# FFN gate and up projections by seven products of quarters, weight sums on the vector engine, and the FFN in three parts

## The chip, the core and the metric

The kernel runs on one core of one Trainium2 chip. A core has a tensor engine (PE: matrix products and transposes, which write to PSUM), a vector engine (DVE), a scalar engine (ACT), GpSimd (POOL) and a sync engine (SP), whose queue issues the transfers here. SBUF is the working memory, PSUM the eight banks in which products are accumulated. The metric is device time in microseconds (us) of one execution; lower is better.

## What is computed

A trunk of two layers over 512 tokens of width 1024, all in float32. Each layer has four sub-layers, each of them normalised before and after and added to the residual stream `h`: a feed-forward network (FFN), a mixer (convolution and gated spatial mixing in layer 0, causal pooling in layer 1), cross-attention over 256 memory tokens, and a second FFN.

```
def swiglu_ffn(h, w_gu, w_down):            # h: 512 x 1024, w_gu: 1024 x 5632, w_down: 2816 x 1024
    gu = h @ w_gu
    gate, up = jnp.split(gu, 2, axis=-1)
    return (jax.nn.silu(gate) * up) @ w_down

for i in range(DEPTH):                      # DEPTH = 2
    f = swiglu_ffn(rms_norm(h, ffn1_pre_g[i]), ffn1_w_gu[i], ffn1_w_down[i])
    h = h + 0.5 * rms_norm(f, ffn1_post_g[i])
    hn = rms_norm(h, mix_pre_g[i])
    m = even_mixer(hn, ...) if i % 2 == 0 else odd_mixer(hn, ...)
    h = h + rms_norm(m, mix_post_g[i])
    c = memory_cross_attention(rms_norm(h, xa_pre_g[i]), mem, ...)
    h = h + rms_norm(c, xa_post_g[i])
    f = swiglu_ffn(rms_norm(h, ffn2_pre_g[i]), ffn2_w_gu[i], ffn2_w_down[i])
    h = h + 0.5 * rms_norm(f, ffn2_post_g[i])
```

## The kernel before, in words

**Split operands.** Every operand of a large product is held as a high part in a short float format (fp32r) and a low part, the exact rest: `split` has ACT write the high part (a cast, L72) and DVE the low part (a subtraction, L73). `mm3` (L75 to L78) then issues three matmuls for one product: high by high, high by low, low by high. Weights come from memory by SP into a `raw` tile (two buffers of 1 MB), and are split into `whi` and `wlo` (five buffers each, `N_W`, of 128 x 1024). Activations lie features-on-partitions in `big` tiles (thirteen buffers).

**Gate and up.** `ffn` goes over 22 blocks of 128 hidden features two at a time. For each pair, `fm_quad` makes four outputs of 128 features by 512 tokens: two of gate, two of up. Each output is eight steps of 128 rows of the weight, each step three matmuls of 512 columns, so 24 matmuls an output and 96 a quad. ACT then takes silu of gate (L322), DVE multiplies by up (L323), and `split` makes the hidden activation. The first quad of a sub-layer runs in two halves of 256 tokens, with the transposes of the later token tiles between them (`pre.turn()`).

**Down.** The hidden features go in two parts, of 12 and of 10 blocks. After the first part, `w_down`'s first twelve blocks are multiplied in: the first 512 output columns are copied to `f`, the second 512 stay open in PSUM (`accs1`). `tm_out` does the last part, with the norm after it: token tile by token tile it squares (L293), scales (L294), adds to `h` (L306), and starts the next sub-layer's norm (`nxt.tile`, `rms_transpose`): square (L127), a root on POOL (L119), scaling by root and gain on DVE (L137), transposes on PE (L144), split. `TAIL` keeps the last eight steps of the second half of the columns in token order, so that the norms of early tiles run under the products of later ones.

**PSUM.** Four banks in pool `pa` (`psa`), two in `pb` (`psb`), two in `pt` (`pst`, and `tps` for transposes).

**Order.** A scheduler sets each engine's order from the program and its estimates of durations; each engine then runs its own list strictly in order, waiting by semaphores for what its instructions need. A tile's buffer is given out again when its last reader has finished.

Of the kernel before, what the change touches and what calls it, by code (L numbers as in the profile page):

```python
# [4 lines left out]
F32 = mybir.dt.float32  # L5
# [5 lines left out]
P = 128  # L11
# [14 lines left out]
N_Q = 3  # L26
N_W = 5
TAIL = 8
CUTS = (0, 4)
TURNS = (0, 2)  # L30


def trunk_kernel(tc, x, mem, ffn1_pre_g, ffn1_w_gu, ffn1_w_down, ffn1_post_g,
# [8 lines left out]
    with ExitStack() as es:  # L42
# [7 lines left out]
        pa = es.enter_context(tc.tile_pool(name="pa", bufs=4, space=bass.MemoryType.PSUM))  # L50
        pb = es.enter_context(tc.tile_pool(name="pb", bufs=2, space=bass.MemoryType.PSUM))
# [9 lines left out]
        # ---------------------------------------------------------- helpers  # L61
# [13 lines left out]
        def mm3(ps, lhs, rhs, start, stop):  # L75
            nc.tensor.matmul(out=ps, lhsT=lhs[0], rhs=rhs[0], start=start, stop=False)  # L76
            nc.tensor.matmul(out=ps, lhsT=lhs[0], rhs=rhs[1], start=False, stop=False)  # L77
            nc.tensor.matmul(out=ps, lhsT=lhs[1], rhs=rhs[0], start=False, stop=stop)  # L78
# [19 lines left out]

        def gain(g, tag):
            gb = gp.tile([P, D], F32, name=tag, tag=tag)  # L100
            nc.sync.dma_start(out=gb, in_=g.partition_broadcast(P))
            return gb

        def gain_by_pe(g, tag):
            """The same spread over partitions by the tensor engine, from one row."""
            row = qt([P, D])
            nc.sync.dma_start(out=row[:1, :], in_=g[None, :])
            one = cst.tile([1, P], F32, name="one")
            nc.vector.memset(one, 1.0)
            gb = gp.tile([P, D], F32, name=tag, tag=tag)  # L110
            for c in (0, 512):
                ps = psb()
                nc.tensor.matmul(out=ps, lhsT=one, rhs=row[:1, c:c + 512], start=True, stop=True)
                nc.vector.tensor_copy(gb[:, c:c + 512], ps)
            return gb
# [6 lines left out]
        def rms_transpose(src, gb, dsts):  # L122
# [17 lines left out]
            def turn():  # L140
                for i in range(2):
# [3 lines left out]
                    split(dsts[i][0], dsts[i][1], tps)  # L145
            return turn

        class Prenorm:
            def __init__(self, g, w, c0s, by_pe=False):
                self.gb = (gain_by_pe if by_pe else gain)(g, "pre")  # L150
                self.x = Act()
                self.turns = []
                self.first = (w, c0s)
                self.ws = None
# [5 lines left out]
            def tile(self, t):  # L160
                self.turns.append(rms_transpose(h[:, t, :], self.gb,
                                                [self.x.block(i, t * P, (t + 1) * P) for i in range(2)]))

            def turn(self):
                self.turns.pop(0)()

# [14 lines left out]
        def w_fm_load(w, c0, parts=1):  # L181
            raw = wp.tile([P, KD, 256], F32, name="raw", tag="raw", bufs=2)
            n = 256 // parts
            return raw, [lambda i=i: nc.sync.dma_start(
                out=raw[:, :, i * n:(i + 1) * n],
                in_=w[:, c0 + i * n:c0 + (i + 1) * n].rearrange("(k p) n -> p k n", p=P)) for i in range(parts)]

        def w_fm(w, c0, raw=None):
# [593 lines left out]
```

## Time and profile before

| | us |
|---|---|
| median of 3 runs (2084.77 to 2086.85) | 2085.42 |
| span of the profiled execution | 2082.8 |
| PE busy in it | 2048.0 (98%) |
| DVE busy | 958.7 (46%) |
| ACT busy | 723.0 (35%) |
| POOL busy | 70.9 (3%) |

The profile is of one execution; its span runs from the first to the last instruction, 2.6 us less than the median time. Matmuls are pipelined, so a matmul's own duration (0.39 us for 512 columns) is longer than the distance from one start to the next, and it is that distance which counts. A group of equal instructions has its count, its busy time and the mean duration of one. An idle time stands with the instruction that ended it.

### The profile page before, as it was taken

The page shows a single profiled execution, that of the slowest core. Times are in us where ns is not written, and L with a number is a line of the kernel's source. Part 1 is how long each engine was busy: PE and PEld are TensorE (multiplying, and loading weights), DVE is VectorE, ACT ScalarE, POOL GpSimd, SP SyncE. Part 2 cuts the span into 40 slices and gives each one's busy share as a digit, 9 for nine tenths or more (in the row PEclk, how much of TensorE's full clock was granted, in tenths as well). Part 3 has the DMA queues.
Part 4 walks back from the last instruction along what each step waited for, and adds up shares of the span by engine and source line. Part 5 has one row for each costly group of instructions (what it writes and reads, how often), then busy time and mean ns, then how long its engine had stood idle before and what let it go on. Part 6 is the DMA issues. An engine that isn't in the chain of part 4 may idle for free.

```text
span 2082.8 us, 24330 instructions
## 1 busy us (share of the span) xinstructions
PE 2048.0 (98%) x10158; PEld 1732.2 (83%) x10158; DVE 958.7 (46%) x1343; ACT 723.0 (35%) x1113; POOL 70.9 (3%) x101
## 2 busy tenths in 40 slices
PE   8999999998999999999999999999999999999998
PEld 7888888887878888888888888888888888888887
DVE  5332233699956463323336332233676654322333
ACT  5222332434454452322224322222444443322221
POOL 0000000112010010000001000000001000000000
PEclk9999999999999999999999999999999999999999
DMA  6223223333632133233223332322352113323221
GB/s 224 85 100 101 90 93 101 118 98 105 224 140 102 66 99 103 98 101 101 96 87 102 102 101 101 101 88 95 102 182 96 67 63 115 97 101 101 98 95 51
DMA packets 165189, 218.17 MB, mean 105 GB/s; under 512 B 3741, under 2 KB 124085, under 8 KB 164056
## 3 DMA queue, kind: packets, MB, share of 16 engines
q1 hardware_dynamic: 163928, 208.24, 30.2%
q0 software_dynamic: 1152, 8.39, 1.0%
q8 instruction: 79, 1.29, 0.3%
q14 instruction: 30, 0.25, 0.0%
HBM read 210.33 MB, written 6.29 MB: 104 GB/s over the span
## 4 chain that ended last, share of the span: by engine, by line
PE 86%; DVE 7%; ACT 2%; POOL 2%; issue 2%; DMA 1%; POOLq 0%; DVEq 0%; ACTq 0%
PE psa L78 13%; PE psa L77 13%; PE psa L76 13%; PE psb L76 11%; PE psb L77 11%; PE psb L78 11%; PE pst L76 4%; PE pst L78 4%; PE pst L77 4%; POOL r L119 1%; DVE q L137 1%; DVE big L483 1%; DVE wlo L73 1%; DVE h L306 1%; PE tps L144 1%
## 5 line engine op out<-in xcount | busy, mean ns | idle before, releaser
L72 ACT CAST whi<-raw 128x1024 fp32r<-128x1024 f32 x370 | 388.1, 1053 | 1114.9 <-PE psb L77 365.9
L73 DVE TENSOR_TENSOR wlo<-raw,whi 128x1024 fp32r<-128x1024 f32 x370 | 452.2, 1225 | 694.9 <-ACT whi L72 686.9
L76 PE MATMUL psb<-big,whi 128*128 128x512 f32 (+1 forms) x1120 | 397.3, 355 | 8.5 <-DVE big L73 8.5
L77 PE MATMUL psb<-big,whi 128*128 128x512 f32 (+1 forms) x1120 | 396.4, 354 | 0.1
L78 PE MATMUL psb<-big,wlo 128*128 128x512 f32 (+1 forms) x1120 | 396.0, 354 | 0.0
L76 PE MATMUL psa<-whi,big 128*128 128x512 f32 x896 | 350.8, 392 | 0.0
L77 PE MATMUL psa<-wlo,big 128*128 128x512 f32 x896 | 349.3, 390 | 0.0
L78 PE MATMUL psa<-whi,big 128*128 128x512 f32 x896 | 348.5, 390 | 0.5 <-DVE big L73 0.5
L76 PEld LDWEIGHTS psb<-big,whi 128*128 128x128 f32 x1120 | 212.7, 190 | 39.5 <-issue 7.8
L77 PEld LDWEIGHTS psb<-big,whi 128*128 128x128 f32 x1120 | 212.8, 190 | 29.3 <-DVE big L73 0.7
L78 PEld LDWEIGHTS psb<-big,wlo 128*128 128x128 f32 x1120 | 212.7, 190 | 28.9
L76 PE MATMUL psa<-big,whi 128*128 128x512 f32 (+1 forms) x656 | 228.6, 349 | 0.0
L78 PE MATMUL psa<-big,wlo 128*128 128x512 f32 (+1 forms) x656 | 228.2, 348 | 0.0
L77 PE MATMUL psa<-big,whi 128*128 128x512 f32 (+1 forms) x656 | 228.1, 348 | 0.0
L78 PEld LDWEIGHTS psa<-whi,big 128*128 128x128 f32 x896 | 168.2, 188 | 35.8 <-DVE big L73 0.9
L76 PEld LDWEIGHTS psa<-whi,big 128*128 128x128 f32 x896 | 168.2, 188 | 35.5 <-ACT big L72 0.8
L77 PEld LDWEIGHTS psa<-wlo,big 128*128 128x128 f32 x896 | 168.2, 188 | 34.1
L78 PEld LDWEIGHTS psa<-big,wlo 128*128 128x128 f32 x656 | 124.1, 189 | 15.6
L76 PEld LDWEIGHTS psa<-big,whi 128*128 128x128 f32 x656 | 124.2, 189 | 15.5
L77 PEld LDWEIGHTS psa<-big,whi 128*128 128x128 f32 x656 | 124.2, 189 | 15.4
L76 PE MATMUL pst<-big,whi 128*128 128x512 f32 x320 | 124.5, 389 | 0.0
L77 PE MATMUL pst<-big,whi 128*128 128x512 f32 x320 | 124.5, 389 | 0.0
(161 smaller groups left out, 1847.0 us busy)
## 6 DMA issues: line engine op xcount, KB each, us to landing
raw<-in_ffn_w_gu_dram SPq DMA_DIRECT2D x86, 1024.0 KB, 5.0
raw<-in_ffn_w_down_dram SPq DMA_DIRECT2D x40, 1024.0 KB, 5.0
raw<-in_xa_w_kv_dram SPq DMA_DIRECT2D x16, 1024.0 KB, 5.4
raw<-in_ev_w_in_dram SPq DMA_DIRECT2D x8, 1024.0 KB, 5.4
raw<-in_xa_w_q_dram SPq DMA_DIRECT2D x8, 1024.0 KB
raw<-in_xa_w_o_dram SPq DMA_DIRECT2D x8, 1024.0 KB, 6.2
raw<-in_ffn_w_down_dram SPq DMA_DIRECT2D x8, 512.0 KB, 3.6
kv<-big POOLq DMA_DIRECT2D x4, 1024.0 KB, 8.0
```

What stands on the lines that cost most here:

```text
L72: nc.scalar.copy(out=hi, in_=src)
L73: nc.vector.tensor_tensor(out=lo, in0=src, in1=hi.bitcast(F32), op=ALU.subtract)
L76: nc.tensor.matmul(out=ps, lhsT=lhs[0], rhs=rhs[0], start=start, stop=False)
L77: nc.tensor.matmul(out=ps, lhsT=lhs[0], rhs=rhs[1], start=False, stop=False)
L78: nc.tensor.matmul(out=ps, lhsT=lhs[1], rhs=rhs[0], start=False, stop=stop)
L119: nc.gpsimd.tensor_tensor(out=r, in0=m, in1=nhalf.broadcast_to([P, n]), op=ALU.pow)
L137: nc.vector.scalar_tensor_tensor(out=xn[:, hs[i]], in0=src[:, hs[i]], scalar=r, in1=gb[:, hs[i]], op0=ALU.mult, op1=ALU.mult)
L144: nc.tensor.transpose(tps[:, k, :], xn[:, (4 * i + k) * P:(4 * i + k + 1) * P], ident)
L306: nc.vector.scalar_tensor_tensor(out=h[:, t, s_], in0=src, scalar=r, in1=h[:, t, s_], op0=ALU.mult, op1=ALU.add)
L483: nc.vector.scalar_tensor_tensor(out=acc[:, c, s_:], in0=z[:, c, :SEQ - s_], scalar=par[:, c, CONV - 1 - s_:CONV - s_], in1=acc[:, c, s_:] ...
```

## The change

For every pair of hidden blocks but an FFN's first, the four outputs are made by seven products instead of eight (Strassen's scheme in Winograd's form). The activation is cut into quarters: tokens in halves of 256, input features in halves of 512. The weight is cut likewise: input features in halves, and gate and up as the two halves of the outputs (256 columns each). `Quarters` keeps the four quarters of the normalised activation, and four sums of them (`ready`, once per FFN, DVE and `split`). `seven` makes four sums of weight quarters on DVE (L310, L313, L318, L321), splits seven weight operands of 128 x 1024, and issues seven products of 24 matmuls with 256 columns, in the order B, A, C, A, C, A, A by the pair of PSUM banks that they use; products to the same pair are accumulated, with copies (ACT) and additions or subtractions (DVE) of the intermediate states between them. In the text below they are P1 to P7.

Beside that: the FFN goes in three parts (8, 8 and 6 blocks), each part's down products are taken out of PSUM and added to two `f` tiles by DVE; the gain of the norm before a sub-layer is applied on DVE after the transposes (L184), per partition, and the scaling by the root moves from DVE to ACT (L175); all gains are loaded as rows and turned once at the start; weights come in pieces of 512 KB into seven `raw` buffers; `whi` and `wlo` have four buffers in place of five; PSUM has six banks in one pool `pa` and two in `pt`; the norm of the memory moves from the first FFN into the mixer of layer 0.

```diff
-N_Q = 3
-N_W = 5
+N_Q = 4
+N_R = 7
+N_W = 4
+FF_PARTS = ((0, 8), (8, 16), (16, NFF))
...
+        class Quarters:
...
+            def ready(self):
+                r0, r1 = self.raws
+                a11, a12, a21, a22 = r0[:, :, :HALF], r1[:, :, :HALF], r0[:, :, HALF:], r1[:, :, HALF:]
+                sub, add = ALU.subtract, ALU.add
+                xs = [ops4() for _ in range(4)]
+                e = qt([P, 4, HALF])
+                for i, (p_, q_, op) in enumerate(((a21, a22, sub), (e, a11, sub), (a12, e, add), (a11, a21, sub))):
+                    if i == 3:
+                        e = qt([P, 4, HALF])
+                    nc.vector.tensor_tensor(out=e, in0=p_, in1=q_, op=op)
+                    split(xs[i][:, 0], xs[i][:, 1], e)
...
-                nc.vector.scalar_tensor_tensor(out=xn[:, hs[i]], in0=src[:, hs[i]], scalar=r,
-                                               in1=gb[:, hs[i]], op0=ALU.mult, op1=ALU.mult)
+                nc.scalar.activation(out=xn[:, hs[i]], in_=src[:, hs[i]], func=AF.Copy, scale=r)
...
-                    split(dsts[i][0], dsts[i][1], tps)
+                    raw = x.raw(i, c0, c1)
+                    nc.vector.tensor_tensor(out=raw, in0=tps, op=ALU.mult,
+                                            in1=g[:, 4 * i:4 * i + 4, None].broadcast_to([P, 4, P]))
+                    hi, lo = x.block(i, c0, c1)
+                    split(hi, lo, raw)
...
+        def seven(w, ca, cb, x, done):
...
+            def product(n, raw, ops, start):
+                wh = parts(raw, (P, 4, 256))
+                for u in range(2):
+                    for k in range(4):
+                        mm3(banks[n][u][:, :HALF], tuple(t_[:, k, u * P:(u + 1) * P] for t_ in wh),
+                            (ops[:, 0, k], ops[:, 1, k]), start and k == 0, k == 3, False)
+                return [b[:, :HALF] for b in banks[n]]
+
+            pb = product("B", b21, x.a12, True)
+            for u, p_ in enumerate(product("A", b11, x.a11, True)):
+                nc.scalar.copy(out=out_a[:, u, lo_h], in_=p_)
+                nc.vector.tensor_tensor(out=out_a[:, u, lo_h], in0=pb[u], in1=out_a[:, u, lo_h], op=ALU.add)
+            nc.vector.tensor_tensor(out=t1, in0=b11, in1=b12, op=ALU.add)
+            for u, p_ in enumerate(product("C", t1, x.x1, True)):
+                nc.scalar.copy(out=out_b[:, u, hi_h], in_=p_)
+            nc.vector.tensor_tensor(out=t1, in0=t1, in1=b22, op=ALU.add)
+            for u, p_ in enumerate(product("A", t1, x.x2, False)):
+                nc.scalar.copy(out=out_b[:, u, lo_h], in_=p_)
+            for u, p_ in enumerate(product("C", b22, x.x4, False)):
+                nc.vector.tensor_tensor(out=out_b[:, u, lo_h], in0=p_, in1=out_b[:, u, lo_h], op=ALU.subtract)
+            nc.vector.tensor_tensor(out=t3, in0=b12, in1=b22, op=ALU.add)
+            for u, p_ in enumerate(product("A", t3, x.x3, False)):
+                nc.vector.tensor_tensor(out=out_b[:, u, hi_h], in0=out_b[:, u, hi_h], in1=p_, op=ALU.subtract)
+            nc.vector.tensor_tensor(out=t1, in0=t1, in1=b21, op=ALU.add)
+            done(out_a, out_b, product("A", t1, x.a22, False))
...
-                    ws = pre.ws if j == 0 else w_fm(w_gu, j * P) + w_fm(w_gu, FF + j * P)
-                    ps = fm_quad([ws[0], ws[2], ws[1], ws[3]], pre, j == 0, pst if j0 else psa)
...
+                    def done(ga, ub, last, j=j):
+                        nc.scalar.activation(out=ga[:, :, :HALF], in_=ga[:, :, :HALF], func=AF.Silu)
+                        for u in range(2):
+                            nc.scalar.activation(out=ga[:, u, HALF:], in_=last[u], func=AF.Silu)
+                        nc.vector.tensor_tensor(out=ga, in0=ga, in1=ub, op=ALU.mult)
+                        ht = hid.put(j - j0)
+                        split(ht[:, 0], ht[:, 1], ga)
+
+                    seven(w_gu, j * P, FF + j * P, pre.x, done)
```

In the gate and up stage, DVE's list before repeats the following, half a quad at a time (`wlo`: a weight's low part; L323: silu of gate times up; `big`: the hidden activation's low part).

```order
L323 TENSOR_TENSOR tmp<-psa,tmp 128x512
L73 TENSOR_TENSOR wlo<-raw,whi 128x1024
L73 TENSOR_TENSOR big<-tmp,big 128x512
L73 TENSOR_TENSOR wlo<-raw,whi 128x1024
L323 TENSOR_TENSOR tmp<-psb,tmp 128x512
```

With the change, DVE's list from P5 of one seven (L317 subtracts its result) to the beginning of the next (L428 is silu of gate times up; L320 takes the state of bank pair A after P6; L310, L318 and L313 are sums of the next seven's weight quarters; q_1922 and q_1923 are its `out_a` and `out_b`) is this.

```order
L317 TENSOR_TENSOR q_1923<-psa,q_1923 128x256 x2
L75 TENSOR_TENSOR wlo<-raw,whi 128x1024
L320 TENSOR_TENSOR q_1923<-q_1923,psa 128x256
L310 TENSOR_TENSOR raw<-raw 128x1024
L320 TENSOR_TENSOR q_1923<-q_1923,psa 128x256
L318 TENSOR_TENSOR raw<-raw 128x1024
L75 TENSOR_TENSOR wlo<-raw,whi 128x1024
L428 TENSOR_TENSOR q_1922<-q_1922,q_1923 128x1024
L313 TENSOR_TENSOR raw<-raw 128x1024
L75 TENSOR_TENSOR big<-q_1922,big 128x1024
L75 TENSOR_TENSOR wlo<-raw,whi 128x1024 x2
```

Where four low parts, two multiplications and two low parts of the hidden activation stood for each quad, there are now seven low parts, four sums, six reads of PSUM, one multiplication and one low part for each seven, and between the two reads of bank pair A after P6 stands a sum.

At the end of the first FFN PE's list before passes from the last products of the down projection (psa_1292) to the first output of the mixer (psb_2665) like this.

```order
L78 MATMUL psa_1292<-whi_2403,big_2167 128x512
L76 MATMUL psb_2665<-big_2442,whi_2609 128x256
L77 MATMUL psb_2665<-big_2443,whi_2609 128x256
L78 MATMUL psb_2665<-big_2442,wlo_2610 128x256
L76 MATMUL psb_2665<-big_2442,whi_2609 128x256
```

With the change the same place in PE's list reads as follows (psa_3466 is the down projection; psa_3730 to psa_3733 are the mixer's first four outputs; whi_3673 and whi_3685 are two different weight tiles).

```order
L81 MATMUL psa_3466<-whi_3481,big_3336 128x512
L79 MATMUL psa_3730<-big_3618,whi_3673 128x256
L79 MATMUL psa_3731<-big_3618,whi_3685 128x256
L79 MATMUL psa_3732<-big_3618,whi_3673 128x256
L79 MATMUL psa_3733<-big_3618,whi_3685 128x256
L80 MATMUL psa_3730<-big_3619,whi_3673 128x256
L81 MATMUL psa_3730<-big_3618,wlo_3674 128x256
```

The first output needed one weight tile for its first steps; now one matmul of each of the four outputs stands first, and the second of them needs a second tile.

## Rows read from the trace of the kernel before

**Rows 1.** The page: span, engines' busy time (share) and instructions.

```profile
span 2082.8 us, 24330 instructions
PE 2048.0 (98%) x10158; PEld 1732.2 (83%) x10158; DVE 958.7 (46%) x1343; ACT 723.0 (35%) x1113; POOL 70.9 (3%) x101
```

**Rows 2.** Stretches: length, busy time (instructions) by engine, PE clock, DMA share, rate.

```profile
core 0: us, PE busy (x) PEld busy (x) DVE busy (x) ACT busy (x) POOL busy (x), PEclk, DMA share, GB/s
4.00:8.00 4.00, 2.21 (x3) 0.33 (x1) 1.66 (x5) 2.67 (x8) 0.55 (x1) 1.00 1.08 348
480.00:500.00 20.00, 12.34 (x92) 12.17 (x91) 20.00 (x28) 5.04 (x6) 0.00 (x0) 0.83 0.43 134
800.00:900.00 100.00, 100.00 (x443) 82.81 (x442) 33.68 (x36) 28.57 (x36) 0.00 (x0) 1.00 0.30 101
```

**Rows 3.** Timeline in a quad: start, duration, engine, line, operation; 24 matmuls lie between.

```profile
100.33 0.39 PE L76 MATMUL psa<-big,whi 128*128 128x512 f32 x1
...
105.55 0.39 PE L78 MATMUL psa<-big,wlo 128*128 128x512 f32 x1
...
105.77 0.39 PE L76 MATMUL psb<-big,whi 128*128 128x512 f32 x1
...
106.04 0.69 DVE L323 TENSOR_TENSOR tmp<-psa,tmp 128x512 f32<-128x512 f32 x1 [3.43 <-PE psa L78]
```

**Rows 4.** Timeline in a first quad, PE: outputs of 256 columns, 24 starts apart.

```profile
405.07 0.28 PE L76 MATMUL psa<-big,whi 128*128 128x256 f32 x1
...
407.95 0.28 PE L76 MATMUL psa<-big,whi 128*128 128x256 f32 x1
```

**Rows 5.** Groups by line and shape: count, busy us, mean ns, idle before.

```profile
L73 DVE TENSOR_TENSOR wlo<-raw,whi 128x1024 fp32r<-128x1024 f32 x370 | 452.2, 1225 | 694.9 <-ACT whi L72 686.9
L72 ACT CAST whi<-raw 128x1024 fp32r<-128x1024 f32 x370 | 388.1, 1053 | 1114.9 <-PE psb L77 365.9 <-PE psa L78 253.0 <-PE psa L77 182.4
L76 PEld LDWEIGHTS psb<-big,whi 128*128 128x128 f32 x1120 | 212.7, 190 | 39.5 <-issue 7.8 <-PE psb L78 1.0 <-ACT big L668 0.8
L72 ACT CAST big<-tmp 128x512 fp32r<-128x512 f32 x92 | 57.1, 621 | 6.0 <-POOL tmp L535 5.4 <-DVE tmp L323 0.6
L323 DVE TENSOR_TENSOR tmp<-psb,tmp 128x512 f32<-128x512 f32 x44 | 30.4, 691 | 140.1 <-PE psb L78 139.4 <-ACT tmp L322 0.7
L668 ACT ACTIVATE q<-psb,mx 128x256 f32<-128x256 f32 x16 | 7.5, 484 | 3.6 <-DVE mx L665 3.6
```

**Rows 6.** Timeline where weights are split back to back, two instructions a row.

```profile
1118.07 2.00 ACT L72 CAST whi<-raw 128x1024 fp32r<-128x1024 f32 x2
...
1120.77 2.35 DVE L73 TENSOR_TENSOR wlo<-raw,whi 128x1024 fp32r<-128x1024 f32 x2
```

**Rows 7.** Timeline at the end of an FFN, PE: the next sub-layer's transposes (L144).

```profile
1111.33 0.39 PE L78 MATMUL psa<-whi,big 128*128 128x512 f32 x1
1111.56 1.03 PE L144 MATMUL tps<-ident,q 128*128 128x128 f32 x8
...
1115.55 0.48 PE L76 MATMUL psa<-whi,big 128*128 128x512 f32 x1
1116.90 0.66 PE L144 MATMUL tps<-ident,q 128*128 128x128 f32 x4 [0.87 <-DVE m L129]
```

**Rows 8.** Waits: engine and line, waited for: us in total, times, longest.

```profile
PE psb L76 <- DVE big L73: 8.5, 2, 7.7
```

**Rows 9.** Timeline of ACT in the mixer of layer 0, at that wait.

```profile
487.92 1.04 ACT L72 CAST whi<-raw 128x1024 fp32r<-128x1024 f32 x1 [8.65 <-DMA raw<-in_xa_w_kv_dram]
```

**Rows 10.** Timeline of the start: first square, second tile's, first product.

```profile
0.81 0.35 SPq L107 DMA_DIRECT2D q<-in_ffn_pre_g_dram  x1
...
4.91 0.63 ACT L127 ACTIVATE q<-h 128x512 f32<-128x512 f32 x1 [2.83 <-DMA h<-in_x_dram]
...
14.22 0.58 PE L76 MATMUL psb<-big,whi 128*128 128x256 f32 x1
```

More of the change, by code (lines that the diff above doesn't have):

```diff
@@ L101, in gain @@
             nc.sync.dma_start(out=gb, in_=g.partition_broadcast(P))
[L102 to L114, printed above, removed]
             return gb
@@ L179, in warm, with raw_tile @@
                 pass
[L181 to L188, printed above, removed]
-            if raw is None:
-                raw, loads = w_fm_load(w, c0)
-                loads[0]()
-            us = []
-            for u in range(2):
-                hi = wp.tile([P, KD, P], F32R, name="whi", tag="whi")
-                lo = wp.tile([P, KD, P], F32R, name="wlo", tag="wlo")
-                split(hi, lo, raw[:, :, u * P:(u + 1) * P])
-                us.append(lambda k, hi=hi, lo=lo: (hi[:, k, :], lo[:, k, :]))
-            return us
+        def raw_tile(shape):
+            return wp.tile(list(shape), F32, name="raw", tag="raw", bufs=N_R)
@@ new lines, in fm_rows, with fm_raw, parts @@
+        def fm_rows(w, i, c0):
+            return w[i * 512:(i + 1) * 512, c0:c0 + 256].rearrange("(k p) n -> p k n", p=P)
+        def fm_raw(w, i, c0):
+            raw = raw_tile([P, 4, 256])
+            nc.sync.dma_start(out=raw, in_=fm_rows(w, i, c0))
+            return raw
+        def parts(raw, shape):
+            hi = wp.tile(list(shape), F32R, name="whi", tag="whi")
+            lo = wp.tile(list(shape), F32R, name="wlo", tag="wlo")
+            split(hi, lo, raw)
+            return hi, lo
@@ L200, in w_tm, with w_fm @@
+        def w_fm(w, c0, raws=None):
+            hl = [parts(raw, (P, 4, 256)) for raw in raws or [fm_raw(w, i, c0) for i in range(2)]]
+            return [lambda k, u=u: tuple(t_[:, k % 4, u * P:(u + 1) * P] for t_ in hl[k // 4]) for u in range(2)]
         def w_tm(w, k0, nk, c0):
-            raw = wp.tile([P, 4, 512], F32, name="raw", tag="raw", bufs=2)
-            nc.sync.dma_start(out=raw[:, :nk, :],
-                              in_=w[k0 * P:(k0 + nk) * P, c0:c0 + 512].rearrange("(k p) n -> p k n", p=P))
@@ L204, in w_tm @@
             us = []
             for u in range(0, nk, 2):
-                hi = wp.tile([P, 2, 512], F32R, name="whi", tag="whi")
-                lo = wp.tile([P, 2, 512], F32R, name="wlo", tag="wlo")
-                split(hi, lo, raw[:, u:u + 2, :])
+                raw = raw_tile([P, 2, 512])
+                nc.sync.dma_start(out=raw, in_=w[(k0 + u) * P:(k0 + u + 2) * P, c0:c0 + 512].rearrange(
+                    "(k p) n -> p k n", p=P))
+                hi, lo = parts(raw, (P, 2, 512))
@@ L259, in tm_out @@
                     mid()
-                if part is None:
-                    accs = [psa() for _ in range(NT)]
-                else:
-                    accs = accs1 if c else [psb(), psb(), pst(), pst()]
-                first = None if c and accs1 else k_order[0]
+                accs = [psa() for _ in range(NT)]
+                first = k_order[0]
                 wk = {}
@@ L287, in tm_out @@
                     sq = tp.tile([P, 512], BF16, name="sq", tag="sq", bufs=1)
[L288 removed]
+                    if part:
+                        dst = part[c][:, t, :]
+                    else:
+                        dst = tp.tile([P, 512], F32, name="tmp", tag="tmp") if c else fg[:, t, :]
                     src = accs[t]
[L290 removed]
+                    if part:
                         src = dst
```

231 lines of the change are left out of this document (141 added, 90 removed).

## The prediction

> **What bounds the kernel now.** I read the busy times first: PE 98%, DVE 46%, ACT 35% [rows 1]. A PE that is busy need not be the bound, since matmuls overlap, so I looked at a stretch of gate and up next: from 800 to 900 us PE is never idle, at the full clock (1.00, the 2.4 GHz level), while DVE works 34 of 100 us and ACT 29 [rows 2]. Then at the distances between starts: 24 matmuls of 512 columns take 105.77 - 100.33 = 5.44 us [rows 3], 0.2267 us each, of which 512 columns at 2.4 GHz are 0.2133. A first quad has the other width: 24 matmuls of 256 columns take 407.95 - 405.07 = 2.88 us [rows 4], 0.120 each, of which the columns are 0.1067. Both widths pay 0.013 us a matmul over the columns. So in the FFNs the number of columns streamed, plus 0.013 us for each matmul, is the time, and the engines beside PE have two thirds of their time free. The reader is to see in rows 3 and 4 that half the columns cost 0.53, not 0.50, of the time.
>
> **What the seven products save.** A quad is 4 x 5.44 = 21.76 us. A seven is 7 products x 24 matmuls x 0.120 = 20.16 us. So not an eighth (2.72 us) is saved but 1.60 us. An FFN has 11 pairs, the first of which stays a quad: 10 sevens x 4 FFNs = 40, and 40 x 1.60 = **64.0 us**. All of this lies on the path, since PE does.
>
> A weight load that is not hidden would turn this round. Rows first: each LDWEIGHTS is recorded at 0.190 us [rows 5], longer than the 0.120 between two starts, and yet every one of the 256-column matmuls has its own and keeps to 0.120 [rows 4]. The Trainium skill, page "TensorE: Matmul & The Clock Gate", says under "LDWEIGHTS (loading the stationary operand)" that a load takes its columns over 1.2 GHz, 107 ns for 128, and in "The mechanism" that it overlaps a running matmul only for another row group. By that rule (an estimate from the page) a 256-column matmul would take 107 + 107 = 213 ns and a seven 36 us; rows 4 contradict it, so it stands below only as a rival.
>
> **What the seven products cost beside PE.** DVE has per seven 7 low parts, 4 weight sums, the multiplication and the low part of the hidden activation: 13 of 128 x 1024 at 1.225 us [rows 5] = 15.9 us. The sums have no row of their own; same shape, operand kinds and engine as the low parts, so the same price. Six reads of PSUM have 256 columns: no row; from 1024 (1.225) and 512 (0.691) [rows 5] a straight line gives 0.42 (bounds 0.35, half of 512, and 0.69). 6 x 0.42 = 2.5. Sum 18.4 us of a 20.16 us seven, 91%. Back to back it is less: two low parts take 2.35 us, so the second starts 1.13 after the first [rows 6], and 13 x 1.13 + 6 x 0.33 = 16.7 us, 83%. ACT: 8 casts x 1.053 = 8.4, six copies and two silus of 256 columns at 0.37 to 0.48 (bounds: the line from 1.053 and 0.621, and the exponential's 0.484), one of 512 at 0.6 [rows 5]: about 12 us, 60%. Both fit under PE, but DVE barely, and it runs its list in order, so the waits count.
>
> I laid one seven out in the order that the list gives, P1 to start at 0, with 0.26 us from the end of a product's slot to the start of its reader (105.55 + 0.227 to 106.04 [rows 3]). Weight buffers number four, so a weight for the product four places on waits for the running one. The tight place is between P5 and P7. P5 ends at 14.40; ACT may overwrite its weight at 14.66 and is done at 15.71; DVE's low part ends at 16.96; only then comes the read of bank A's first half after P6 (L320), to 17.3, while P7 wants that bank at 17.28. Then DVE does a sum (1.13), and the second read ends at 18.75 against 18.72. So P7 is late by some 0.1 us and PE's restart: I take 0.15 us a seven, with 0 (the scheduler put enough ahead) and 0.6 (full durations in place of start distances give 0.33, and as much again for the restarts) as bounds. P1 to P4 of the next seven have 2 to 3 us in hand in the same layout. Behind a DVE that waits at L320 stand the next seven's sums and low parts; they are needed 6 us later. 40 x 0.15 = **+6 us** (0 to +24).
>
> **Entering an FFN.** `ready` gives DVE 4 x (1.13 + 1.13) = 9 us within the first quad, which is 23 us on PE. It fits, but L310 and the third low part come behind L418, which waits for the quad's end; cast, hidden low part, two sums, cast, low part after that end at 31.5 when P3 wants its weight at 30.6. About +1.5 us each (0 to 3.5): 4 x 1.5 = **+6**.
>
> **Boundaries of sub-layers.** Seven times PE passes from a sub-layer's last products to the next one's first. Now the transposes wait some there: the second set starts 0.87 us late [rows 7], and all in all some 1.7 us are lost at each. The change moves 1.4 us of scaling from DVE to ACT, which helps the first set, but puts a DVE multiplication of 0.69 between transposes and cast, ahead of each split, and adds DVE's addition (L374) in the FFN's second half of columns. In an FFN the tail has six steps in place of eight, 4.08 us a token tile for 5.44. And PE's list begins with a matmul that needs a second weight tile, whose cast stands behind the cast of the activation: two casts (2 x 1.05) after PE is done in place of one. I take +1.7 each (0.4 to 3): **+12** (+3 to +21).
>
> **Start, mixer, end.** At the start six small loads (0.35 us each on SP's queue [rows 10]) come before x, and x's second half behind 2 MB of weights in place of 1 MB; at 348 GB/s [rows 2] 1 MB more is 3 us. The first squares move from 4.9 to 6.8 us, and two more operations (gain, cast) stand on the way to the first product, now at 14.2 [rows 10]: **+4** (+2 to +7). In layer 0's mixer PE waited 7.7 us once [rows 8] for a low part out of a `psb` bank, behind an ACT that waited 8.65 us for a weight load [rows 9], and in that stretch the clock fell to 0.83 [rows 2]. Seven half-size `raw` buffers start that load earlier, and six banks in place of two take away the wait; but DVE is never idle there [rows 2], so what it owes comes due later, and one weight buffer less and the memory's norm (some 8 us of ACT, which has the time) come in. **-4** (-10 to +6). The parts of the FFN cost nothing: while the down products of a part run, a weight tile lasts PE 5.44 us and DVE less than 2 of them. The last token tile has one addition more: **+1**.
>
> **Sum.** 2082.8 - 64.0 + 6 + 6 + 12 + 4 - 4 + 1 = 2043.8 for the span, and 2.6 us more outside it, as now (2085.4 is the median): **2046 us**. With the bounds added by halves (not all at one end), 2034 to 2060.
>
> **Rivals.**
> *Half the gain is handed back in the sevens.* If the two reads after P6 come 0.4 us later each (the low part before them starts on a later release, or 256 columns out of PSUM cost near 0.69), P7 starts 0.4 late twice: 0.8 a seven in place of 0.15, +26 us: 2072. For it: the margin there is under 0.1 us. Against it: start distances are shorter than durations throughout the trace.
> *DVE sets the pace of a seven.* Then its 18.4 us do not lie side by side with its waits: for P7 and silu (1.1 us after what it does meanwhile), and for three buffers in PE's hands (0.9, 0.5 and 0.7 in my layout with full durations): 21.5 us or more, a gain of 0.2 us x 40 = 10 at most, and entries, boundaries, start and end take 23: 2097 us. It decides from 21.2 us a seven on. For it: 91% by durations, in one strict list. Against it: the waits are for events that come at PE's pace, and the layout had 2 us and more in hand everywhere else.
> *The small costs are hidden.* No loss in the sevens and entries, boundaries +4, mixer -7: 2082.8 - 64 + 4 + 4 - 7 + 1 + 2.6 = 2023 to 2034. For it: PE lost nothing at all in 100 us of FFN [rows 2].
> *Weight loads unhidden at 256 columns.* If each load of 0.190 [rows 5] stood ahead of its 0.107 of columns, a seven would be 50 us, and the kernel 1100 us slower. The page's rule named above is of this kind. Rows 4 exclude it for the same instruction.
>
> **How the numbers follow.** The forecast (2034 to 2060) has 0.65, half handed back 0.15, DVE's pace 0.09, hidden costs 0.10, unhidden loads 0.01. A measurement of this kernel can tell 0.2%, 4 us. Faster: the forecast, hidden costs and most of the half-way case, 0.87; same 0.03; slower 0.10. The range that holds 8 in 10 takes the forecast's, the near part of the hidden costs and most of the half-way case: 2030 to 2074.
>
> **What would show it.** In the profile after: 256-column starts at 0.120 within the sevens and 20.2 to 20.4 us from one P1 to the next; DVE near 85% and ACT near 60% in a stretch of sevens; PE's waits in a seven short and all at P7, released by L320. DVE above 95% there, with waits at P3 or P4 too, would show the second rival. Waits of 1 to 3 us at P3 of an FFN's first seven and 3 to 4 us at the boundaries would show the other terms. The layout is wrong if the order of events in it is: if a sum or a cast is late by more than a product's 2.88 us.

## The result and the profile after

The changed kernel takes 2063.79 us (median; 2059.15 to 2064.23) against 2085.38 for the kernel before on the same chip: 0.989 of it, 95% interval 0.9876 to 0.9904. It is faster by 21.6 us. The forecast was a gain of 39 us, to 2046. The range, 2030 to 2074, held the time; the likeliest case's own range, 2034 to 2060, missed it by 4 us.

The page of the changed kernel, span and engines, answers to [rows 1]:

```profile
span 2062.5 us, 31671 instructions
PE 2000.3 (97%) x13033; PEld 1830.5 (89%) x13033; DVE 1415.6 (69%) x1855; ACT 991.8 (48%) x1565; POOL 80.1 (4%) x101
```

There are 2875 more matmuls recorded and yet 20.3 us less span. PE's share fell from 98 to 97%: that is the loss to look for. First the inside of the FFN, against the third row of [rows 2] (length, then busy us and instructions of PE, PE's loads, DVE, ACT, POOL, then PE's clock): 100 us of sevens with the down products of one part between them, and below it one seven alone. Then DVE's timeline from one seven's sum L310 to the next:

```profile
800.00:900.00 100.00, 100.00 (x664) 92.51 (x664) 59.04 (x61) 45.95 (x66) 0.00 (x0) 1.00 0.33 105
801.18:821.38 20.20, 20.20 (x171) 20.20 (x170) 17.36 (x21) 11.31 (x18) 0.00 (x0) 1.00 0.32 106
```

```profile
799.71 1.22 DVE L310 TENSOR_TENSOR raw<-raw 128x1024 f32<-128x1024 f32 x1
...
813.55 1.23 DVE L75 TENSOR_TENSOR wlo<-raw,whi 128x1024 fp32r<-128x1024 f32 x1 [1.11 <-ACT whi L74]
...
819.58 0.41 DVE L320 TENSOR_TENSOR q<-q,psa 128x256 f32<-128x256 f32 x1
819.91 1.22 DVE L310 TENSOR_TENSOR raw<-raw 128x1024 f32<-128x1024 f32 x1
821.04 0.41 DVE L320 TENSOR_TENSOR q<-q,psa 128x256 f32<-128x256 f32 x1
```

PE is never idle there, the clock is full, a seven lasts 819.91 - 799.71 = 20.20 us, and in the second row DVE works 17.36 of 20.20 us (86%), ACT 11.31 (56%). The seven products do what the sum of columns says.

So the loss is elsewhere. I added up, over all of PE's starts, what exceeds the pitch of the matmul's width (0.227 us for 512 columns, 0.120 for 256, 0.109 for a transpose), once for each kernel, and parted it by stretches, counting also the time ahead of PE's first start and behind its last. The first row of the table is no such sum: it is the matmuls counted, times these pitches.

| | forecast | measured |
|---|---|---|
| columns: 3840 of 512 out, 6720 of 256 in | -64 | -65.3 |
| inside the sevens | +6 | +1.5 |
| entries of the FFNs, four | +6 | +10.4 |
| boundaries of sub-layers, seven | +12 | +27.7 |
| start | +4 | +5.2 |
| mixer of layer 0 | -4 | -3.2 |
| mixer of layer 1 | 0 | +4.4 |
| cross-attention | 0 | -2.3 |
| end | +1 | +1.8 |
| sum | -39 | -19.8 |

The spans themselves differ by 20.3 us.

The boundaries are most of the gap, 15.7 of 19.2 us. Four of the seven hold nearly all of it: the ends of three FFNs (+7.5, +6.5, +5.9) and of the first mixer (+6.7). This is the end of layer 0's second FFN, engine by engine (start, duration; in brackets the idle time ahead and what ended it), where [rows 7] shows the kernel before:

```profile
1109.97 3.67 POOL L158 TENSOR_TENSOR r<-m,nhalf 128x1 f32<-128x1 f32 x1 [2.92 <-DVE m L171]
```

```profile
1109.68 0.15 DVE L171 SCALAR_TENSOR_TENSOR m<-ss,m 128x1 f32<-128x1 f32 x1
1109.74 3.49 DVE L75 TENSOR_TENSOR wlo<-raw,whi 128x1024 fp32r<-128x1024 f32 x3
```

```profile
1113.67 1.33 ACT L175 ACTIVATE q<-h,r 128x512 f32<-128x512 f32 x2 [3.44 <-POOL r L158]
```

```profile
1107.17 0.38 PE L79 MATMUL psa<-big,whi 128*128 128x256 f32 x1 [0.54 <-ACT big L74]
1108.12 0.63 PE L79 MATMUL psa<-big,whi 128*128 128x256 f32 x3 [0.56 <-ACT whi L74]
1109.15 0.39 PE L80 MATMUL psa<-big,whi 128*128 128x256 f32 x1 [0.41 <-DVE m L168]
...
1114.45 0.65 PE L182 MATMUL tps<-ident,q 128*128 128x128 f32 x4 [3.12 <-ACT q L175]
```

Read it backwards. PE waits 3.12 us for the scaling on ACT, ACT 3.44 us for the root on POOL, and the root, one column, takes 3.67 us where it mostly takes 0.55. While it runs, DVE does three low parts without a pause, from 1109.74 to 1113.23, and the root ends 0.41 us behind the last. The other ends show 3.67, 3.20 (end of the mixer) and 3.67 us. Behind the wait the clock falls (same columns as above, then two of PE's rows):

```profile
1110.00:1114.00 4.00, 1.33 (x12) 1.13 (x10) 3.23 (x3) 0.56 (x2) 3.64 (x1) 1.00 0.45 136
1114.00:1118.00 4.00, 3.55 (x19) 3.52 (x20) 2.45 (x5) 2.64 (x6) 0.00 (x0) 0.63 0.77 261
```

```profile
1116.19 0.41 PE L81 MATMUL psa<-big,wlo 128*128 128x256 f32 x1
1116.40 0.41 PE L79 MATMUL psa<-big,whi 128*128 128x256 f32 x1
```

0.63 of 2.4 GHz is a mix of the two levels, 1.2 and 2.4 GHz, and the starts from 1116.19 to 1118.11 are 0.21 us apart, the pitch at 1.2 GHz, in place of 0.12. Over the whole span such distances cost some 15 us after and some 5 before.

### The profile page after: what moved, and what is told of

Same layout as the page of the kernel before. It is cut to its first block, busy times and chain, and to the rows that moved or that the text cites. A ratio compares the mean times of both kernels' runs of the same rounds, so it can differ in the third digit from the quotient of the medians.

```text
span 2062.5 us, 31671 instructions
## 1 busy us (share of the span) xinstructions
PE 2000.3 (97%) x13033; PEld 1830.5 (89%) x13033; DVE 1415.6 (69%) x1855; ACT 991.8 (48%) x1565; POOL 80.1 (4%) x101
## 4 chain that ended last, share of the span: by engine, by line
PE 83%; DVE 7%; issue 4%; ACT 3%; POOL 2%; DMA 0%; SPq 0%; DVEq 0%; POOLq 0%; ACTq 0%
PE psa L79 27%; PE psa L80 27%; PE psa L81 27%; DVE wlo L75 2%; POOL r L158 2%; PE tps L182 1%; DVE big L582 1%; DVE big L75 1%; DVE h L388 1%; ACT q L175 1%; ACT whi L74 1%; ACT sq L375 0%; DVE big L483 0%; DVE tmp L376 0%; ACT big L74 0%
## 5 line engine op out<-in xcount | busy, mean ns | idle before, releaser
L79 PE MATMUL psa<-big,whi 128*128 128x256 f32 (+1 forms) x3056 | 888.7, 293 | 13.2 <-ACT big L74 7.9
L81 PE MATMUL psa<-big,wlo 128*128 128x256 f32 (+1 forms) x3056 | 885.5, 291 | 10.3 <-DVE wlo L75 10.3
L75 DVE TENSOR_TENSOR wlo<-raw,whi 128x1024 fp32r<-128x1024 f32 x490 | 594.5, 1222 | 430.6 <-ACT whi L74 430.1
L80 PE MATMUL psa<-big,whi 128*128 128x256 f32 (+1 forms) x3056 | 886.8, 291 | 1.5 <-DVE m L168 0.9
L74 ACT CAST whi<-raw 128x1024 fp32r<-128x1024 f32 x490 | 511.1, 1050 | 631.6 <-PE psa L81 287.1
L79 PEld LDWEIGHTS psa<-big,whi 128*128 128x128 f32 x3056 | 587.2, 193 | 26.3 <-ACT big L74 13.3
L81 PEld LDWEIGHTS psa<-big,wlo 128*128 128x128 f32 x3056 | 588.0, 193 | 19.4 <-DVE wlo L75 12.3
L80 PEld LDWEIGHTS psa<-big,whi 128*128 128x128 f32 x3056 | 588.5, 193 | 10.9 <-DVE big L75 3.7
L79 PE MATMUL psa<-whi,big 128*128 128x512 f32 x1056 | 413.4, 392 | 1.2 <-DVE tmp L633 1.2
L81 PE MATMUL psa<-whi,big 128*128 128x512 f32 x1056 | 411.3, 390 | 0.0
L74 ACT CAST big<-q 128x1024 fp32r<-128x1024 f32 x62 | 64.7, 1050 | 79.4 <-DVE q L428 62.7
L75 DVE TENSOR_TENSOR big<-q,big 128x1024 fp32r<-128x1024 f32 x62 | 75.5, 1223 | 14.5 <-ACT big L74 14.5
L582 DVE SCALAR_TENSOR_TENSOR big<-big,par 128x511 f32<-128x511 f32 (+29 forms) x120 | 85.2, 766 | 0.0
L175 ACT ACTIVATE q<-h,r 128x512 f32<-128x512 f32 x64 | 42.7, 715 | 25.1 <-POOL r L158 24.1
```

The source lines that it names most:

```text
L74: nc.scalar.copy(out=hi, in_=src)
L75: nc.vector.tensor_tensor(out=lo, in0=src, in1=hi.bitcast(F32), op=ALU.subtract)
L175: nc.scalar.activation(out=xn[:, hs[i]], in_=src[:, hs[i]], func=AF.Copy, scale=r)
L582: nc.vector.scalar_tensor_tensor(out=acc[:, c, s_:], in0=z[:, c, :SEQ - s_], scalar=par[:, c, CONV - 1 - s_:CONV - s_], in1=acc[:, c, s_:] ...
```

## The theories

**A.** POOL's root is held up by DVE's low parts, because the change took the scaling off DVE. Before, DVE's own next work at this place (the scaling, L137) needed the root, so DVE waited for POOL; now nothing there does, and the list is filled with low parts. The kernel before at this place, POOL's root and the scaling that waits for it:

```profile
1111.44 0.55 POOL L119 TENSOR_TENSOR r<-m,nhalf 128x1 f32<-128x1 f32 x1 [2.48 <-DVE m L132]
1112.02 1.42 DVE L137 SCALAR_TENSOR_TENSOR q<-h,r,pre 128x512 f32<-128x512 f32 x2 [0.66 <-POOL r L119]
```

**B.** The boundaries lose what the new steps on the path take (gain behind the transposes, two casts ahead of PE's first products). **C**, for the entries: the split of the first pair's hidden activation stands ahead of the third product's weight. **D**: the four sums of `ready` set it.

The Trainium skill, page "SBUF — State Buffer", section "Who interferes with whom", has the rule behind A: a DVE instruction with two SBUF inputs contends with a GpSimd instruction that reads SBUF, and the loser blocks. The trace of the kernel before agrees, with little harm: six of its roots take 1.40 us, each beside one low part of 1.22, as here. The prediction did not weigh it.

```profile
1127.16 1.22 DVE L73 TENSOR_TENSOR wlo<-raw,whi 128x1024 fp32r<-128x1024 f32 x1
1127.39 1.40 POOL L119 TENSOR_TENSOR r<-m,nhalf 128x1 f32<-128x1 f32 x1 [2.92 <-DVE m L132]
```

## The experiments

**The seven products undone, with their quarters and sums; the other edits kept** (`quads`).

```diff
-            return Prenorm(col(n, l), w[l], (0, FF), True)
+            return Prenorm(col(n, l), w[l], (0, FF))
...
-                    seven(w_gu, j * P, FF + j * P, pre.x, done)
+                    ws = pre.ws if j == 0 else w_fm(w_gu, j * P) + w_fm(w_gu, FF + j * P)
+                    ps = fm_quad([ws[0], ws[2], ws[1], ws[3]], pre, j == 0)
...
```

> All pairs of all FFNs are made by quads of 512 columns again, without quarters and sums; three parts, seven half-size buffers, the gain behind the transposes, the order at the boundaries and the start stay as in the changed kernel. Theory A (the loss at the boundaries belongs to the rest of the change): 65 us of columns come back, some 9 of the entries and 2 in the sevens go: 2064 + 65 - 11 = 2118, and POOL's roots of over 3 us stay at the boundaries. Rival (it belongs to the seven products and their tiles): the boundaries cost as before the change, and the time is 2085 to 2098.

2126.38 us, 1.0192 of the kernel before (1.0177 to 1.0208). The kernel is 2126.4 - 2063.8 = 62.6 us slower without the sevens, and the rest of the change by itself costs 40.6. That 62.6 is near the 65.3 of the columns is in part chance: 2118 was expected, since the entries' loss goes with the sevens. It did go (some 10 us by the sum of starts), but two more roots, at the ends of both cross-attentions, are held here, and these two boundaries lose 7.7 us each, where they lose 2.3 and 2.5 in the changed kernel, by the same sum. So the held roots are there without any seven, six of over 3 us. One is at an end of an FFN, one at the end of an attention:

```profile
1141.93 3.67 POOL L158 TENSOR_TENSOR r<-m,nhalf 128x1 f32<-128x1 f32 x1 [2.92 <-DVE m L171]
767.46 3.20 POOL L158 TENSOR_TENSOR r<-m,nhalf 128x1 f32<-128x1 f32 x1 [3.46 <-DVE m L171]
```

**The root on DVE** (`root_vec`).

```diff
-            nc.gpsimd.tensor_tensor(out=r, in0=m, in1=nhalf.broadcast_to([P, n]), op=ALU.pow)
...
+            nc.vector.tensor_scalar(out=nh, in0=m, scalar1=-0.5, scalar2=None, op0=ALU.mult)
...
+            nc.vector.tensor_scalar(out=y, in0=m.bitcast(I32), scalar1=1, scalar2=None,
+                                    op0=ALU.logical_shift_right)
...
+            nc.vector.tensor_scalar(out=g, in0=y, scalar1=-1.0, scalar2=float(0x5f3759df),
+                                    op0=ALU.mult, op1=ALU.add)
...
+            for i in range(3):
...
+                nc.vector.scalar_tensor_tensor(out=t, in0=g, scalar=nh, in1=g, op0=ALU.mult, op1=ALU.mult)
...
+                nc.vector.scalar_tensor_tensor(out=y, in0=t, scalar=1.5, in1=g, op0=ALU.add, op1=ALU.mult)
```

> The root of each mean square is worked out on DVE, by nine operations on one column (three Newton steps), in place of the power on POOL; roots of several columns stay on POOL. Theory A (at four boundaries POOL's root is held up for 3.2 to 3.7 us by DVE operations with two operands in SBUF that follow each other, and the clock falls behind PE's wait): the waits of 2.2 to 3.1 us before the transposes near 376, 628, 1111 and 1470 us fall below 1 us, the granted clock there stays near 1.00, and the time falls by 12 to 20 us, to 2044 to 2052. Theory B (the loss at the boundaries is made of the new steps on the path, the gain's multiplication and a second cast): the waits stay above 2 us and the time stays within 4 us of the changed kernel's 2064.

2131.38 us, 67.6 slower than the changed kernel: a miss, and no test of A, since it puts another wait in the place. The nine operations, most of which need the one before, take 1.76 us (from 1142.96 to 1144.72), and with them the lists came out in another order; PE's waits in the whole span:

```profile
PE tps L200 <- ACT q L193: 56.0, 15, 9.3
```

**Next weights split later** (`warm_late`), an order alone.

```diff
                         tm_part(accs, a, wk, tail[at:], first, k_order[-1], [t])
-                        if t == 3:
-                            nxt.warm()
...
                     nxt.tile(t)
+                    if t == 3 and tail:
+                        nxt.warm()
```

> The next sub-layer's first weights are split behind the last token tile's norm in the program, not ahead of it. On DVE's list an addition that reads PSUM (0.68 us) now follows the third tile's mean square, and only then come two weight low parts; before it three low parts followed at once. Theory A (hold of POOL's root): with one operand in PSUM next to it the root takes 0.55 to 0.9 us in place of 3.7, PE's longest wait at the boundaries falls from 3.1 to under 1.5 us, and the time falls by 8 to 16 us, to 2048 to 2056. Theory B (new steps on the path): the waits keep their size or grow, since the weights' casts come later; 2062 to 2070.

2051.91 us, 0.9838 (0.9823 to 0.9853): 12 us better than the changed kernel. At the same end of the FFN, POOL's root, DVE's operation beside it, PE's waits from 1095 to 1160 us (us in total, times, longest; the first of them lies in the entry behind), and the clock of the stretch behind the root:

```profile
1105.60 0.55 POOL L158 TENSOR_TENSOR r<-m,nhalf 128x1 f32<-128x1 f32 x1 [2.92 <-DVE m L171]
1105.37 0.69 DVE L372 TENSOR_TENSOR big<-psa,big 128x512 f32<-128x512 f32 x1
```

```profile
PE psa L81 <- DVE wlo L75: 1.7, 1, 1.7
PE psa L79 <- ACT whi L74: 1.0, 2, 0.6
PE psa L79 <- ACT big L74: 0.5, 1, 0.5
PE psa L80 <- DVE m L168: 0.4, 1, 0.4
```

```profile
1106.00:1110.00 4.00, 4.00 (x25) 4.00 (x25) 4.00 (x7) 2.47 (x5) 0.41 (x2) 0.65 0.40 107
```

An addition that reads PSUM (0.69 us) now lies beside the root, the root takes 0.55, and the wait for the scaling is gone. What stays, 0.4 to 0.6 us each, are B's casts and the restart behind them, and behind these short waits alone the clock still falls, to 0.65. At the end of the first mixer the root is held as before, 3.20 us.

**A read of the root ahead of the low parts** (`guard`), which takes the hold away at every boundary.

```diff
             r = rsqrt(m2)
+            seen = sm.tile([P, 1], F32, name="seen", tag="seen", bufs=2)
+            guard = nc.vector.tensor_copy(out=seen, in_=r)
...
-                        if t == 3:
-                            nxt.warm()
+                        if t == 3 and isinstance(nxt, Prenorm):
+                            with tc.issue_after(nxt.guard):
+                                nxt.warm()
```

> DVE reads each token tile's root once (a copy of one column, new), and the low parts of the next sub-layer's first weights stand on its list behind that copy; nothing else is edited. Theory A (hold of POOL's root by low parts that follow each other): the roots of 3.2 to 3.7 us at the four boundaries become 0.55 to 0.9 us, PE's wait before the transposes there falls by some 2.5 us and the clock's fall behind it goes too: 2064 - 4 x (2.5 + 1) = 2050, between 2046 and 2056. Theory B (new steps on the path): PE still waits above 2 us there; 2062 to 2070, since the low parts come a microsecond later.

2057.64 us, 0.9866 (0.9853 to 0.988): 6 us of the 14 expected, just outside the range that A gave. No root is over 1.0 us any more, and from 600 to 650 us, at the end of the mixer, what exceeds the pitch fell from 9.2 to 5.4 us. At the FFN's ends another wait has come in its place (PE's waits at the end of layer 0's second FFN, then DVE's and ACT's rows):

```profile
PE psa L79 <- ACT big L74: 3.1, 1, 3.1
PE tps L184 <- ACT q L177: 0.8, 1, 0.8
```

```profile
1103.19 1.41 DVE L392 SCALAR_TENSOR_TENSOR h<-big,r,h 128x512 f32<-128x512 f32 x2 [0.44 <-POOL r L158]
1104.52 0.68 DVE L186 TENSOR_TENSOR big<-tps,cols 128x512 f32<-128x512 f32 x1
1105.26 1.25 ACT L74 CAST big<-big 128x512 fp32r<-128x512 f32 x2
```

PE waits 3.1 us for the cast of the second tile's activation. On ACT's list it now stands behind the squares of the third tile, which end at 1105.36, and the gain's multiplication that it reads (L186) stands on DVE's list behind the additions to `h` (L392) and ends at 1105.20. Both lists were reordered by the edit.

**The scaling back on DVE** (`scale_dve`), one part of the change undone.

```diff
-                nc.scalar.activation(out=xn[:, hs[i]], in_=src[:, hs[i]], func=AF.Copy, scale=r)
+                nc.vector.tensor_scalar(out=xn[:, hs[i]], in0=src[:, hs[i]], scalar1=r, scalar2=None, op0=ALU.mult)
```

> One part of the change undone: the scaling by the root goes back from ACT to DVE (two operations of one operand and a scalar, 128x512, a token tile); the gain stays behind the transposes. On DVE's list the scaling now stands between the third tile's mean square and the low parts, and it needs the root, so DVE itself waits for POOL there. Theory A (the hold, let in because nothing on DVE's list waited for the root any more): roots of 3.2 to 3.7 us vanish, PE's waits of 2.2 to 3.1 us before the transposes go, 2064 falls by 6 to 12 us to 2052 to 2058, as far as no other wait takes their place. Theory B (new steps on the path at the boundary): scaling on DVE adds 1 us a tile to its list, waits stay, 2064 to 2070.

2052.53 us, 0.984 (0.9827 to 0.9854): 11 us came back, at the upper end of what A said. Not all of it need be the hold: the scaling itself is shorter on DVE, 0.88 us a token tile for 1.33 on ACT. POOL's roots, as a group, mean 623 ns for 776 in the changed kernel and 633 before. The scaling, then the roots:

```profile
1093.06 0.88 DVE L175 TENSOR_SCALAR q<-h,r 128x512 f32<-128x512 f32 x2
```

```profile
L158 POOL TENSOR_TENSOR r<-m,nhalf 128x1 f32<-128x1 f32 x74 | 46.1, 623 | 1834.1 <-DVE m L384 1658.4 <-DVE m L171 100.7 <-DVE m L535 56.1
```

Most of it came at the end of the first mixer (2.9 us above the pitch for 9.2, from 600 to 650 us); at the three FFN ends a wait of 3.2 us for the activation's cast took the root's place here too.

**The hidden activation split behind the first seven** (`defer_split`).

```diff
-                        ht = hid.put(j - j0)
-                        split(ht[:, 0], ht[:, 1], s_)
+                        held = s_
                         continue
...
                     seven(w_gu, j * P, FF + j * P, pre.x, done)
+                    if j == 2:
+                        ht = hid.put(0)
+                        split(ht[:, 0], ht[:, 1], held)
```

> The first pair's hidden activation is split behind the first seven in the program, not ahead of it. Theory C (at an FFN's entry the third product's weight is late because the hidden activation's cast and low part, 1.05 + 1.13 us, stand ahead of it): PE's waits in an FFN's first seven fall from some 2.3 us to below 1 us, four times, and the time falls by 4 to 7 us, to 2057 to 2060. Theory D (the four sums of the activation's quarters and their splits, 9 us of DVE, set it): the waits stay above 2 us, the time within 2 us of 2064.

2059.07 us, 0.9872 (0.9856 to 0.9889): 4.7 us better. PE's waits from 762 to 800 us, first in the changed kernel, then here:

```profile
PE psa L81 <- DVE wlo L75: 1.7, 1, 1.7
PE psa L79 <- ACT whi L74: 0.4, 1, 0.4
```

```profile
PE psa L79 <- ACT whi L74: 0.7, 2, 0.5
```

C holds and D is out for this wait: the wait for the third product's low part is gone with the four sums still there, and what is left is shorter than 1 us. By the sum of starts the entries still lose 5.6 us, about half of what they lost; that rest was not parted.

**Together.** `late_defer` is `warm_late` with `defer_split`.

> The next sub-layer's first weights are split behind the last tile's norm (2051.9 when alone) and the first pair's hidden activation behind the first seven (2059.1 when alone, 4.7 less than the changed kernel). Sum of both by addition: 2047. If both draw on the same wait: 2050 to 2052.

2047.20 us, 0.9815 (0.9801 to 0.9828): the sum of both, as two causes at two places give. `guard_defer` is `guard` with `defer_split`:

> The same, and the first pair's hidden activation is split behind the first seven. If the two causes lie at different places (boundaries, entries), the gains add: guard's time less 4 to 6 us, 2042 to 2050. If the hidden activation's later split only moves work into DVE's path at the boundary or elsewhere: guard's time within 2 us.

2053.36 us (0.9833 to 0.986): 4.3 less than `guard`, again the sum. `late_defer_guard` adds the read of the root to `late_defer` at the ends of mixers and attentions alone, and `late_defer_scale` adds the scaling on DVE:

```diff
-                    nxt.tile(t)
+                    nxt.tile(t, part is None and t == 2)
                     if t == 3 and tail:
-                        nxt.warm()
+                        if part is None:
+                            with tc.issue_after(nxt.guard):
+                                nxt.warm()
+                        else:
+                            nxt.warm()
```

> The two reorderings (2047.2 together), and at the four ends of a mixer and of an attention DVE reads the third tile's root ahead of the next weights' low parts. If the one root still held for 3.2 us (near 623) costs PE its 2.2 us of wait and the clock behind it: 2043 to 2045. If another wait takes its place, as a wait for the activation's cast did when such reads stood at all boundaries (2057.6): 2047 to 2050.

> The same with the two reorderings of before (next weights split behind the last tile's norm, first pair's hidden activation behind the first seven; 2047.2 together). If the roots that are still held there (3.2 us near 623, 1.4 us at six places) cost PE time: 2040 to 2045. If they are hidden by now: 2047 within 2 us, or slower by the scaling's time on DVE's list in the mixers, up to 2052.

2043.78 us, 0.9797 (0.9783 to 0.981), and 2044.84 us, 0.9802 (0.9789 to 0.9816), which can't be told from each other. Both beat the changed kernel by some 20 us and the kernel before by some 2%. The mean clock of `late_defer_guard` is 0.996 to 0.999 in its executions, where the changed kernel has 0.992 to 0.994. `late_defer` still has one root of over 2 us, at the end of the first mixer; first there, then with the read of it:

```profile
623.29 3.20 POOL L158 TENSOR_TENSOR r<-m,nhalf 128x1 f32<-128x1 f32 x1 [3.46 <-DVE m L171]
622.49 0.98 POOL L158 TENSOR_TENSOR r<-m,nhalf 128x1 f32<-128x1 f32 x1 [3.46 <-DVE m L171]
```

There, from 600 to 650 us, what exceeds the pitch fell by 2.8 us, most of the 3.4 us between the two kernels, as the expectation for one held root said (2043 to 2045).

**The hold by itself** (`hold` and `hold3`).

```diff
+                nc.gpsimd.tensor_tensor(out=r, in0=a[:, 0:1], in1=nhalf, op=ALU.pow)
+                for op in plan:
+                    op()
```

> A kernel of its own that computes nothing of the trunk and writes the input to the output: POOL's root of one column is started just ahead of a chain of DVE operations, once for each chain: none; 1, 2, 3 and 6 subtractions with two operands in SBUF of 1024 columns; 3 of 512; 3 multiplications with one operand in PSUM; subtraction and PSUM multiplication by turns, 3 each; 3 operations of one SBUF operand; 3 of two SBUF operands and a scalar; 3 copies on ACT. Theory A (a chain of operations with two SBUF operands holds POOL to its end): the root takes some 0.55 us with none, with PSUM operands and beside ACT, and 1.4, 2.5, 3.7 and 7 us with 1, 2, 3 and 6 subtractions; by turns it gets in at the first PSUM operation, 1.4 us. If POOL is held for one operation only: 1.4 us for every length. If DVE doesn't hold POOL: 0.55 us throughout.

> A kernel of its own that computes nothing of the trunk, as hold, but DVE's operations of a chain write three tiles by turns, so that each can start before the one ahead of it has ended, as the low parts do in the trunk (starts 1.13 us apart, 1.22 long). In hold, where all wrote one tile (starts 1.25 apart), the root took 1.59 us for 1, 2, 3 and 6 subtractions alike. If POOL gets in wherever DVE's reads pause: 1.6, 2.5, 3.7 and 7 us for 1, 2, 3 and 6 here. If POOL waits for one operation of DVE at most: 1.6 us for each, and what held the roots for 3.7 us in the trunk must be something else.

The root in `hold` beside, in this order, one subtraction, six of them, three multiplications with an operand in PSUM, three operations of two SBUF operands and a scalar, and nothing:

```profile
9.06 1.59 POOL L86 TENSOR_TENSOR r<-a,nhalf 128x1 f32<-128x1 f32 x1 [3.10 <-DVE a L84]
...
17.73 1.59 POOL L86 TENSOR_TENSOR r<-a,nhalf 128x1 f32<-128x1 f32 x1 [2.45 <-DVE a L84]
...
27.99 0.55 POOL L86 TENSOR_TENSOR r<-a,nhalf 128x1 f32<-128x1 f32 x1 [1.39 <-DVE a L84]
...
39.09 0.55 POOL L86 TENSOR_TENSOR r<-a,nhalf 128x1 f32<-128x1 f32 x1 [1.03 <-DVE a L84]
...
46.82 0.55 POOL L86 TENSOR_TENSOR r<-a,nhalf 128x1 f32<-128x1 f32 x1 [2.94 <-DVE a L84]
```

and in `hold3` beside six subtractions that overlap:

```profile
16.85 1.59 POOL L92 TENSOR_TENSOR r<-a,nhalf 128x1 f32<-128x1 f32 x1 [2.20 <-DVE a L90]
```

A subtraction with two SBUF operands holds the root, an operation with one of them in PSUM doesn't: that much of the rule behind A agrees. The three operations of two SBUF operands and a scalar did not hold it, though by that rule they should have. And in these kernels the root waits for one subtraction only, however long the chain, so that A's 3.7 and 7 us for three and six fell. In the trunk it waited for three.

## Why the prediction was right, and where it was not

- **What bounds the kernel, and what the sevens save.** Right: a seven lasts 20.20 us for 20.16, and the columns counted are worth -65.3 for -64.0. That the kernel is 62.6 us slower with its quads back agrees, though two effects of some 10 us cancel in it. The rival of unhidden weight loads is out: the 168 matmuls of a seven, each with its load, take 20.20 us and PE is never idle.
- **Inside the sevens.** Too high: +1.5 for +6. The tight place at P7 showed no wait; DVE had 14% to spare. Neither of the two rivals that put the loss there happened. The rival at 2072 came nearer the time than the forecast did, for a reason that did not occur; and since the range reached up to 2074 for that rival's sake, it is luck that it held the time. The other rival's 2097 does not add up: 2085.4 - 10 + 23 is 2098, and 2094 with the mixer's -4.
- **Entries.** The step was right, the third product's weight behind the hidden activation's split, and `defer_split` shows it for 4.7 us. It was mis-sized: 10.4 for 6.
- **Boundaries.** This term failed: +27.7 for +12, above its bound of 21. The prediction took the move of the scaling to ACT as something that "helps the first set", and priced the casts and the gain's multiplication. The casts are there at 0.5 to 0.6 us each. What it missed is that the scaling on DVE had kept DVE's low parts away from POOL's root. `scale_dve`, which undoes that one edit, gives back 11 us. It also left out the clock: at the four bad boundaries distances at half clock are some 7 us after and some 1 before.
- **How much is A.** Taking the hold away brought 6 us (`guard`) or 11 (`scale_dve`), not the 15.7 by which the term was short, because at the FFN's ends a wait of some 3 us for a cast came in its place. An order in which neither occurs there (`warm_late`) brought 12. Where one root of 3.20 us was left and taken away (`late_defer_guard`), 3.4 us went with it. So hold and order of the lists at the boundary make up the gap together, and their shares can't be parted cleanly.
- **Start, mixer of layer 0, end.** Within 1.2 us each. At the start the first squares come at 6.77 us, as forecast (6.8). In the mixer of layer 0 the wait of 7.7 us is gone and six waits for weights' low parts, 4.5 us together, have come in: what DVE owes did come due later. The mixer of layer 1 (+4.4) had no term; its one long wait, 2.7 us at 1531.47 for a cast of the activation, was not tried.

## What to carry to other kernels

Before moving a step off an engine, ask who waited for something because of it: a wait on one engine's list can be what keeps that engine's other work out of a third engine's way. Waits of PE cost more than their length where the clock falls behind them, so price them with the clock: here it fell to 0.63 behind a wait of 3.1 us that followed three short ones, and to 0.65 behind three of 0.4 to 0.6 us alone. And when a wait is taken away, look for the one that takes its place: here a wait of 3.1 us for a cast came for one of 3.1 us for a root.

## What was not expected of the hardware

- The root of one column on POOL, 0.55 us, took 3.67 us beside three DVE subtractions in a row. In a kernel of its own it took 1.59 us beside one, two, three or six. Why it waited for three in the trunk stays open. One difference is that it started 0.16 to 0.23 us behind the first subtraction there and 0.05 us here, but that alone does not decide how many it waits for. These two, in `warm_late` and in `late_defer_guard`, both start 0.22 to 0.23 us behind a low part of 1.22 us, which a second of 0.68 follows without a pause; the first root ends 0.41 us behind the first of them, the second 0.41 us behind the second:

```profile
631.18 1.40 POOL L158 TENSOR_TENSOR r<-m,nhalf 128x1 f32<-128x1 f32 x1 [4.01 <-DVE m L382]
1565.29 2.00 POOL L158 TENSOR_TENSOR r<-m,nhalf 128x1 f32<-128x1 f32 x1 [5.07 <-DVE m L390]
```

- DVE operations of two SBUF operands and a scalar (1.32 us each) did not hold it in `hold`: 0.55 us. In the changed kernel's mixer of layer 0 one of 0.74 us (L582) did: the root at 408.13 took 0.98 us, and there it had started later, 0.17 us behind. In `hold`, operations with one SBUF operand, 0.69 us each for 1024 columns, did: 1.41 us.
- In a seven PE starts a matmul of 256 columns every 0.120 us with a weight load each (168 in 20.20 us) at full clock.
